# Modulation transfers on SyncE from the used weight tile, and one loop in the general path

## The chip, the cores and the metric

The kernel runs on one core of a Trainium2 chip. The metric is the device time of one execution in microseconds (us); the time shown is the median of three runs. All data are f32. Engines are named as in the profile: PE (TensorE), DVE (VectorE), ACT (ScalarE), POOL (GpSimd), SP (SyncE).

## What is computed

Two models in a row, on 256 tokens of width 1024. The first has two layers, each an attention mixer and a mixture of 16 experts (MoE). The second has one layer of another mixer and another MoE, and it is modulated by a vector c:

```python
mod = jax.nn.silu(c) @ w_ada[l] + b_ada[l]
sh1, sc1, g1, sh2, sc2, g2 = jnp.split(mod, 6, axis=-1)
h = _rms(x, norm1_g[l]) * (1.0 + sc1[:, None, :]) + sh1[:, None, :]
...
for e in range(N_EXPERTS):
    a = jax.nn.silu(h @ w_gate[e]) * (h @ w_up[e])
    y = y + dense_gates[:, e:e + 1] * (a @ w_down[e])
```

w_ada is 1024 x 6144. It needs c alone, so its product can be made at any time before the second model. Each expert has a gate and an up matrix of 1024 x 512 and a down matrix of 512 x 1024, 2 MB each, so a MoE loads 96 MB of weights. A token goes to two experts.

## The kernel before, in words

`run` (L1835) emits the program in this order: loads, then twice mixer (L572), router and `moe` (L955); then mixer2 (L1340), its router and `moe`. The order of the instructions on every engine is the order in which the Python code writes them.

**The weights.** Every weight load is a DMA issued by SP in `wload` (L109 to L115, the issue is L114). A `w` tile is 8 KB in each partition, 1 MB in all, and the pool has 13 of them; others come from pools r, b, 4 and 2. `moe_loads` cuts a MoE's weights into 96 jobs of 1 MB: by pairs of experts, gate, up and down, two halves of each expert. The function `load(upto)` issues the jobs that are not issued yet, up to a number. LATE (L35) is (3, 21): job 3, the second half of the gate of the first pair's second expert, is taken out of its place and becomes the 22nd; it comes as four pieces of 256 KB.

**Where the loads stand.** In a mixer, `filler` (L671) goes through the string FILL[l] (L30), one step at a time, between the units of attention:

```python
FILL = ("qkvcfgh5xaoAoAoAopppp", "qkvcfgh5xaoAoAoAoApppp")
MOE_FIRST = 22, 21
ADA_MX, ADA_TR = ((0, 1, 2, 3), (4, 6, 7, 8, 9), (11,)), (5, 10)
```

'5' is load(5), the first five expert jobs. 'x' loads the residual and the out projection's weights w_o, 'a' the further modulation weights `wa`, 'o' and 'p' are out projections (L541, into pout), and 'A' is one step of the modulation. In `moe`, load(MOE_FIRST[blk]) (L1014) issues the first 22 jobs (21 in the second model), as far as they are not issued; the general path (`overflow`) and load((0, 2)) follow. Then come eight pairs: expand (L1019, the products pz at L1026 with gate and up), shrink of the pair before (L1061, py at L1073 with down), gather and scatter, load((pr+1, 2)), and an ada step (L1119, L1120).

**The modulation.** `ada` (L1230 to L1263) makes w_ada's product in 12 blocks of 512 columns, each from two `wa` tiles. `rows(j)` (L1240) makes pada in PSUM; ACT copies pada to `part` (L1259, L1260), a tile of the m2 pool; `keep` (L1244) sends one row in 32 of part to a DRAM tile `ada`, by a DMA on the ACT queue (L1250). Once both halves of a segment are there, `column` (L1265) is put into a queue, and it reads the segment back as columns `adac` by another DMA on ACT's queue (L1268); `total` (L1271), on DVE, adds up and comes two ada steps after it. Blocks 0 to 3 belong to mixer 0: three by 'A', and the last in `run` by `next(fill, None)` (L1880), ahead of the call of `moe`. Block 5 comes after MoE 1, blocks 4, 6, 7, 8, 9 in mixer 1 (four by 'A' and the last at L1880), block 10 after MoE 2, block 11 in mixer2.

**The m2 pool.** It has five places of 2 KB in each partition (L81). `part` shares them with the softmax's E (written by ACT at L442), its transpose PT (L137), G (L975), sil, act, aT and the four pieces of job 3.

**The general path.** `overflow` (L1124) reads a flag that DVE made from the counts of tokens by expert. Only if an expert has more than 64 tokens does it go through all experts without the packing, in tiles lent by two of the loaded jobs, under the branch of L1128. In the profiled execution no instruction of that path ran, only the branch.

The functions that the change touches, and what calls them:

Of the kernel before, what the change touches and what calls it, by code (L numbers as in the profile page):

```python
# [10 lines left out]
F32 = mybir.dt.float32  # L11
# [4 lines left out]
AF = mybir.ActivationFunctionType  # L16
ALU = mybir.AluOpType
# [5 lines left out]
P = 128  # L23
# [24 lines left out]
class Net:  # L48
# [513 lines left out]
    def out_loads(self, src, pools, js):  # L562
# [7 lines left out]
        return t  # L570

    def mixer(self, l, hT, parts, W, ada, mid, tr, load):  # L572
        nc, c = self.nc, self.c

# [96 lines left out]
        def filler():  # L671
# [5 lines left out]
            for step in FILL[l]:  # L677
                if step in steps:
                    yield from steps[step]()
                    if step == "k" and l == 0:  # L680
                        self.tables2()
                    elif step == "f" and l == 0:
                        self.spread1()
                    elif step == "h" and l == 0:
                        self.spread2()
                elif step == "c":
                    fox_cum()
                    yield
                elif step == "a":
                    W["ada"] += self.ada_loads(ADA_MX[l][ADA_1[l]:])  # L690
                elif step in "123456789":
                    load(int(step))
                elif step == "x":
                    xt.append(self.unspill(xd, "xres"))
                    W["wo"] += self.out_loads(self.A["p_w_out"][l], OUT[0][0], OUT[0][2])
                elif step == "A":
                    next(ada, None)
                    yield
                else:
                    i = "op".index(step)  # L700
                    if not acc[i]:
                        acc[i] = [self.ps("pout", t) for t in ("aa", PT1)[i]]
                    for n in range(2):
                        self.out_mm(acc[i][n], oT, W["wo"], i, n, cc[i], cc[i] + 1)
                    cc[i] += 1
                    yield
# [417 lines left out]
    def overflow(self, parts, g, b, W, flag, gov, yacc, colscale, places, again):  # L1124

        nc, c = self.nc, self.c
        v = nc.values_load(flag[0:1, 0:1], min_val=0, max_val=1)
        with self.tc.If(v > 0):  # L1128
            govd = self.dp.tile([P, 32], F32, name="govd")
            nc.gpsimd.dma_start(govd, gov.rearrange("p i e -> p (i e)"))  # L1130
            for i in range(2):
                hT = [x.rearrange("p (k t) -> p k t", k=4) for x in places[:2]]
                for k in range(8):
                    pt = self.ps("opt", "t")
                    for n, part in enumerate(parts):
                        nc.tensor.matmul(pt[:, :P], part[:, i, k, :].bitcast(F32), c["ident"],
                                         start=(n == 0), stop=(n == 1))
                    self.evac(hT[k // 4][:, k % 4, :], pt[:, :P], g[:, k:k + 1], b[:, k:k + 1])
                with self.tc.For_i(0, 16) as e:
                    w3 = W(bass.ds(e, 1))  # L1140
                    gc = places[7][:, 0:1]
                    nc.gpsimd.dma_start(gc, govd[:, bass.ds(e + 16 * i, 1)])
                    pz = []
                    for n in range(2):
                        z = self.ps("oz", "a")
                        src = w3[n].rearrange("o (p k) f -> p (o k) f", k=8)
                        for k in range(8):
                            w = places[2 + k % 2]
                            nc.gpsimd.dma_start(w, src[:, k, :])
                            nc.tensor.matmul(z, hT[k // 4][:, k % 4, :], w, start=(k == 0), stop=(k == 7))  # L1150
                        pz.append(z)
                    a = places[4]
                    nc.scalar.activation(a, pz[0], AF.Silu)
                    nc.vector.tensor_mul(a, a, pz[1])
                    pa = self.ps("opa", "t")
                    for f in range(4):
                        nc.tensor.transpose(pa[:, f * P:(f + 1) * P], a[:, f * P:(f + 1) * P], c["ident"])
                    aT = places[5].rearrange("p (f t) -> p f t", f=4)
                    nc.scalar.activation(aT.rearrange("p f t -> p (f t)"), pa, AF.Copy)
                    src = w3[2].rearrange("o (c p) f -> p (o c) f", p=P)  # L1160
                    for n in range(2):
                        py = self.ps("opy", "o")
                        s = slice(n * 512, (n + 1) * 512)
                        for f in range(4):
                            w = places[2 + f % 2]
                            nc.gpsimd.dma_start(w, src[:, f, s])
                            nc.tensor.matmul(py, aT[:, f, :], w, start=(f == 0), stop=(f == 3))
                        if colscale is None:
                            nc.vector.scalar_tensor_tensor(yacc[:, i, s], py, gc, yacc[:, i, s], op0=ALU.mult,
                                                           op1=ALU.add)  # L1170
                        else:
                            t = places[6]
                            nc.vector.scalar_tensor_tensor(t, py, gc, colscale[:, s], op0=ALU.mult, op1=ALU.mult)
                            nc.vector.tensor_add(yacc[:, i, s], yacc[:, i, s], t)
            for t, src in again:
                nc.gpsimd.dma_start(t, src)
# [53 lines left out]
    def ada(self, blocks, W, tag="t", late=False):  # L1230


        nc, c = self.nc, self.c

        def rows(j):
            pa = self.ps("pada", tag)
            for k4 in range(2):
                w = W[2 * j + k4]
                for k in range(4):
                    nc.tensor.matmul(pa[32 * k:32 * k + 32, :], c["cz"][:, 4 * k4 + k:4 * k4 + k + 1].to_broadcast([P, 32]), w[:, k, :],  # L1240
                                     start=(k4 == 0), stop=(k4 == 1), tile_position=(0, 32 * k), skip_group_check=True)
            return pa

        def keep(b, part):  # L1244

            seg, n = divmod(b, 2)
            whole = seg in self.adad
            if not whole:
                self.adad[seg] = self.dp.tile([4, D], F32, name=f"ada{seg}")
            nc.scalar.dma_start(self.adad[seg][:, n * 512:(n + 1) * 512], part[::32, :])  # L1250
            if whole:
                self.adaq += [lambda: None, lambda: self.column(seg)]

        for j, b in enumerate(blocks):
            self.ada_step()
            pa = rows(j)
            if late:
                yield
            part = self.m2([P, 512], "part")  # L1259
            nc.scalar.activation(part, pa, AF.Copy)  # L1260
            keep(b, part)
            yield
        yield  # L1263

    def column(self, seg):  # L1265
        nc, c = self.nc, self.c
        r = self.adac[seg] = self.m1([P, 4, 8], "adac")
        nc.scalar.dma_start(r, self.adad[seg].rearrange("r (q k) -> q r k", k=8))  # L1268
        self.adaq += [lambda: None, lambda: self.total(seg)]

    def total(self, seg):  # L1271
# [808 lines left out]
```

## Time and profile before

| what | value |
|---|---|
| median of three runs | 1252.47 us (1248.62 to 1252.79) |
| profiled execution | 1256.93 us |
| its span | 1255.3 us |
| PE busy | 1168.0 us, 93% of the span |
| DVE, ACT, POOL busy | 515.8, 381.8, 223.6 us |
| mean granted clock of PE | 0.974 |
| moved by DMA | 395.51 MB, mean 315 GB/s |
| last scatter product of MoE 1 ends on PE | 406.85 us |
| branch L1128 on PE (three times) | 2.685, 6.027, 6.050 us |

The span is the profiled stretch of the execution; its own time is 1.6 us more. Times inside the execution count from the start of the span. "Granted clock" is the TensorE clock that the throttle granted, as a share of full speed. An "issue" is the instruction with which an engine hands a DMA to a queue; its landing comes later. In a row of a timeline, "x4" is the number of instructions of one kind that are put together, and the bracket tells how long the engine was idle ahead of the first and which event ended that.

### The profile page before, as it was taken

How to read it: one execution, taken by the hardware profiler on the slowest of the kernel's cores; microseconds unless marked ns; L12 is line 12 of the kernel's file. 1: busy time of each engine (PE TensorE's matmuls, PEld its weight loads, DVE VectorE, ACT ScalarE, POOL GpSimd, SP SyncE). 2: the span in 40 equal slices, each digit the busy share in tenths (PEclk: the TensorE clock that was granted, in tenths of full speed). 3: DMA queues.
4: the chain of work that ended last, by engine and by line, in shares of the span. 5: the costliest groups of instructions: out<-in, count | busy, mean ns of one | idle time of the engine just before them, and what ended most of it. 6: DMA issues, size and time to landing. Idle time of an engine off the chain costs nothing. (4 is left out here: it accounts for less than half of the span.)

```text
span 1255.3 us, 16639 instructions
## 1 busy us (share of the span) xinstructions
PE 1168.0 (93%) x6360; PEld 675.0 (54%) x6366; DVE 515.8 (41%) x1135; ACT 381.8 (30%) x799; POOL 223.6 (18%) x320
## 2 busy tenths in 40 slices
PE   5999798999999899987999999789899998999997
PEld 4877353434443788535344343388898553434432
DVE  6665342212222656425023221465886351223323
ACT  5544332111111655415011011356455431101100
POOL 4653200000000356200000000022564200000000
PEclk9999899999999999988999999989899998999999
DMA  9815939999999963757899999984344358999995
GB/s 384 353 40 210 384 116 368 415 411 404 415 417 413 390 245 135 306 198 277 344 373 417 414 414 416 417 337 166 108 169 155 147 226 314 415 415 415 415 417 231
DMA packets 80895, 395.51 MB, mean 315 GB/s; under 512 B 10760, under 2 KB 12528, under 8 KB 52384
## 3 DMA queue, kind: packets, MB, share of 16 engines
q1 hardware_dynamic: 73488, 384.66, 77.1%
q10 hardware_dynamic: 7312, 9.62, 2.2%
q8 instruction: 55, 0.90, 0.3%
q14 instruction: 40, 0.33, 0.1%
HBM read 389.41 MB, written 6.51 MB: 315 GB/s over the span
## 5 line engine op out<-in xcount | busy, mean ns | idle before, releaser
L1026 PE MATMUL pz<-we,xT 128*64 128x512 f32 x1536 | 342.3, 603 | 14.4 <-PEq L1128 13.2
L1026 PEld LDWEIGHTS pz<-we,xT 128*64 128x64 f32 x1536 | 111.0, 139 | 232.4 <-issue 223.8
L1073 PE MATMUL py<-wd,aT 128*64 128x512 f32 x768 | 173.3, 593 | 3.0 <-DMA wd<-in_exp_w_down 2.1
L1035 DVE TENSOR_TENSOR act<-sil,pz 128x512 f32<-128x512 f32 x24 | 16.5, 688 | 320.5 <-PE pz L1026 295.5
L1073 PEld LDWEIGHTS py<-wd,aT 128*64 128x64 f32 x768 | 55.5, 137 | 115.7 <-issue 106.5
L1050 POOL TENSOR_SCALAR m_ge<-m_s 64x1 f32<-64x1 f32 x48 | 11.9, 249 | 587.6 <-DVE m_s L1045 334.3
L1079 ACT ACTIVATE yh<-py,m_ge 128x512 fp32r<-128x512 f32 x32 | 22.0, 687 | 191.9 <-PE py L1073 191.9
L1030 ACT ACTIVATE sil<-pz 128x512 f32<-128x512 f32 x24 | 14.3, 597 | 210.9 <-PE pz L1026 202.1
L1080 DVE SCALAR_TENSOR_TENSOR yl<-py,m_ge,yh 128x512 fp32r<-128x512 f32 x32 | 24.0, 751 | 101.0 <-ACT yh L1079 101.0
L541 PE MATMUL pout<-w_o,oT 128*128 128x512 f32 x128 | 61.1, 627 | 4.7 <-ACT part L1260 4.7
L986 PE MATMUL pg<-G,xhi 128*128 128x256 f32 x192 | 47.8, 290 | 2.0 <-DVE G L975 2.0
L448 POOL TENSOR_SCALAR E<-E,r 128x128 f32<-128x128 f32 x40 | 30.7, 767 | 105.4 <-DVE r L444 101.6
L986 PE MATMUL pg<-G,xlo 128*128 128x256 f32 x192 | 46.7, 283 | 0.0
L541 PEld LDWEIGHTS pout<-w_o,oT 128*128 128x128 f32 x128 | 24.9, 203 | 32.7 <-issue 27.2
L1085 ACT ACTIVATE yh<-yf 128x512 fp32r<-128x512 f32 x16 | 10.1, 630 | 104.0 <-DVE yf L1084 104.0
L1099 PE MATMUL psc<-yh,GT 128*128 128x512 f32 x96 | 39.3, 410 | 1.1 <-ACT yh L1085 0.8
L1101 DVE TENSOR_TENSOR yacc<-yacc,psc 128x512 f32<-128x512 f32 x64 | 40.1, 680 | 0.0
L1099 PE MATMUL psc<-yl,GT 128*128 128x512 f32 x96 | 38.5, 401 | 1.3 <-DVE yl L1080 0.6
L986 PEld LDWEIGHTS pg<-G,xhi 128*128 128x128 f32 x192 | 36.7, 191 | 2.4 <-issue 1.6
L442 ACT ACTIVATE E<-s,nm 128x128 f32<-128x128 f32 (+1 forms) x48 | 20.2, 421 | 56.1 <-DVE nm L441 42.3
L986 PEld LDWEIGHTS pg<-G,xlo 128*128 128x128 f32 x192 | 36.8, 191 | 0.0
L291 PE MATMUL pt<-pk,xn 128*128 128x128 f32 x96 | 17.1, 337 | 12.3 <-ACT xn L132 12.2
(498 smaller groups left out, 2107.9 us busy)
## 6 DMA issues: line engine op xcount, KB each, us to landing
wd<-in_exp_w_down SPq DMA_DIRECT2D x58, 1024.0 KB, 12.7
we<-in_exp_w_up SPq DMA_DIRECT2D x54, 1024.0 KB, 11.9
we<-in_w SPq DMA_DIRECT2D x52, 1024.0 KB, 14.7
we<-in_exp_w_gate SPq DMA_DIRECT2D x48, 1024.0 KB, 13.9
wd<-in_w SPq DMA_DIRECT2D x29, 1024.0 KB, 17.3
wa<-in_p_ada SPq DMA_DIRECT2D x24, 1024.0 KB, 12.4
we<-in_exp_w_gate SPq DMA_DIRECT2D x28, 512.0 KB, 13.0
we<-in_w SPq DMA_DIRECT2D x22, 512.0 KB, 13.7
```

Of the source, the lines that this page charges most:

```text
L291: nc.tensor.transpose(pt[:, k * P:(k + 1) * P], xn[:, 4 * k4 + k, :], self.c["ident"])
L442: nc.scalar.activation(E[:, s], sc[:, s], AF.Exp, bias=nm[:, i:i + 1], accum_out=sm[:, i:i + 1])
L448: self.nc.gpsimd.tensor_scalar(E[:, 0:P], E[:, 0:P], r[:, 0:1], None, op0=ALU.mult)
L541: self.nc.tensor.matmul(acc, oT[:, cc, i * P:(i + 1) * P], w[cc][:, n * 512:(n + 1) * 512], start=(cc == 0), stop=(cc == 7), skip_group_ch ...
L986: nc.tensor.matmul(pg[:, :256], part[:, i, k, :], Gq[q][:, i].rearrange("p e s -> p (e s)"), start=(n == 0), stop=(n == 3))
L1026: nc.tensor.matmul(pz[64 * e:64 * e + 64, :], x[:, k, o + 64 * e:o + 64 * e + 64], w[e][k], start=(k == 0), stop=(k == 7), skip_group_chec ...
L1035: nc.vector.tensor_mul(a, st[pr].pop("sil"), pz)
L1073: nc.tensor.matmul(py[n][64 * e:64 * e + 64, :], aT[:, f, 64 * e:64 * e + 64], w[e][f][:, n * 512:(n + 1) * 512], start=(f == 0), stop=(f ...
L1079: nc.scalar.activation(yh[:, s], py[n], AF.Copy, scale=ge)
L1080: nc.vector.scalar_tensor_tensor(yl[:, s], py[n], ge, yh[:, s].bitcast(F32), op0=ALU.mult, op1=ALU.subtract)
L1099: nc.tensor.matmul(pt, GT[:, i * P:(i + 1) * P], y[:, s], start=(j == 0), stop=(j == 1), skip_group_check=True)
L1101: nc.vector.tensor_tensor(yacc[:, i, s], yacc[:, i, s], pt, op=ALU.add)
```

## The change

Three edits. In the general path the loop over the experts takes both tiles of tokens in its body, where before it was written out once for each; the tokens' parts are added by DVE first and then transposed. In `ada` the copied product goes into the first of the four 512-wide rows of the second `wa` tile that `rows` has just used, where before it had an m2 tile of its own. And keep's and column's DMAs are issued by SP, where before ACT issued them.

```diff
@@ overflow @@
+            for i in range(2):
+                for j in range(2):
+                    k = slice(4 * j, 4 * j + 4)
+                    nc.vector.tensor_tensor(x[2 * i + j], parts[0][:, i, k].bitcast(F32), parts[1][:, i, k].bitcast(F32),
+                                            op=ALU.add)
             for i in range(2):
-                hT = [x.rearrange("p (k t) -> p k t", k=4) for x in places[:2]]
                 for k in range(8):
                     pt = self.ps("opt", "t")
-                    for n, part in enumerate(parts):
-                        nc.tensor.matmul(pt[:, :P], part[:, i, k, :].bitcast(F32), c["ident"],
-                                         start=(n == 0), stop=(n == 1))
...
-                with self.tc.For_i(0, 16) as e:
-                    w3 = W(bass.ds(e, 1))
-                    gc = places[7][:, 0:1]
-                    nc.gpsimd.dma_start(gc, govd[:, bass.ds(e + 16 * i, 1)])
+                    nc.tensor.transpose(pt[:, :P], x[2 * i + k // 4][:, k % 4, :], c["ident"])
...
+            gc = self.sp.tile([P, 2, 1], F32, name="m_gc", bufs=1)
+            with self.tc.For_i(0, 16) as e:
+                w3 = W(bass.ds(e, 1))
+                nc.gpsimd.dma_start(gc, govd.rearrange("p (i e) -> p i e", i=2)[:, :, bass.ds(e, 1)])
+                for i in range(2):
...
@@ keep @@
-            nc.scalar.dma_start(self.adad[seg][:, n * 512:(n + 1) * 512], part[::32, :])
+            nc.sync.dma_start(self.adad[seg][:, n * 512:(n + 1) * 512], part[::32, :])
@@ ada @@
-            part = self.m2([P, 512], "part")
+            part = W[2 * j + 1][:, 0, :]
             nc.scalar.activation(part, pa, AF.Copy)
@@ column @@
-        nc.scalar.dma_start(r, self.adad[seg].rearrange("r (q k) -> q r k", k=8))
+        nc.sync.dma_start(r, self.adad[seg].rearrange("r (q k) -> q r k", k=8))
```

## Rows read from the trace of the kernel before

**Rows 1.** Windows: busy us of PE, PEld, DVE, ACT, POOL; clock, DMA share, GB/s

```profile
118.00:153.00 35.00, 26.11 (x132) 12.56 (x131) 10.47 (x32) 10.48 (x35) 7.53 (x11) 0.89 0.98 393
...
300.00:400.00 100.00, 100.00 (x486) 40.56 (x484) 23.38 (x45) 13.71 (x21) 1.91 (x8) 1.00 1.02 412
700.00:804.00 104.00, 101.46 (x482) 40.91 (x478) 26.50 (x52) 14.48 (x22) 1.91 (x8) 1.00 1.02 415
```

**Rows 2.** Waits: engine, line, releaser, total us, times, longest

```profile
ACT E L442 <- DMA ada<-part: 21.0, 5, 8.2
...
PE pz L1026 <- PEq L1128: 13.2, 3, 5.6
```

**Rows 3.** Timeline of ACT: start, us, work, [idle before, releaser]

```profile
134.78 0.37 ACT L442 ACTIVATE E<-sd,nm 128x128 f32<-128x128 f32 x1 [8.24 <-DMA ada<-part]
...
191.94 0.51 ACTq L1250 DMA_DIRECT2D ada<-part  x1
...
584.43 0.49 ACTq L1250 DMA_DIRECT2D ada<-part  x1
```

**Rows 4.** Timeline of PE, five windows, same columns

```profile
137.82 1.22 PE L525 MATMUL hss<-hsq,bones 128*128 128x256 f32 x2 [6.06 <-ACT hsq L516]
...
141.11 2.22 PE L1240 MATMUL pada<-wa,cz 128*32 128x512 f32 x16
...
150.68 0.52 PE L455 MATMUL ptp<-pk,E 128*128 128x128 f32 x3 [1.85 <-DVE PT L137]
...
199.88 6.12 PE L1026 MATMUL pz<-we,xT 128*64 128x512 f32 x18 [2.17 <-PEq L1128]
206.95 5.37 PE L1026 MATMUL pz<-we,xT 128*64 128x512 f32 x24 [0.94 <-DMA we<-in_exp_w_gate]
...
542.22 6.53 PE L541 MATMUL pout<-w_o,oT 128*128 128x512 f32 x8 [4.71 <-ACT part L1260]
...
595.63 15.68 PE L1026 MATMUL pz<-we,xT 128*64 128x512 f32 x64 [5.43 <-PEq L1128]
```

**Rows 5.** Windows after two stops of PE

```profile
149.00:156.00 7.00, 5.32 (x20) 3.19 (x21) 3.23 (x10) 2.80 (x11) 1.51 (x2) 0.76 0.97 350
542.20:549.00 6.80, 6.78 (x10) 3.04 (x11) 1.69 (x6) 1.79 (x6) 1.30 (x2) 0.58 0.97 351
```

**Rows 6.** Timeline of SP (DMA issues) in mixer 0

```profile
115.60 3.09 SPq L114 DMA_DIRECT2D wa<-in_p_ada  x4
120.93 13.46 SPq L114 DMA_DIRECT2D we<-in_exp_w_up  x2
```

**Rows 7.** Tile views, landing: we (43 to 60), wa (114 to 196)

```profile
DMA to landing us min/median/max: 5.0/5.1/5.1
...
DMA to landing us min/median/max: 23.3/23.3/23.3
```

**Rows 8.** DMA from 120.5 to 191.8: GB/s in slices, issues

```profile
GB/s 439 414 439 421 409 425 418 421 267 313 386 432 418 411 404 363 359 301 395 345 379 216 101 7 9 0 0 0 0 0 0 0 64 322 202 106 381 414 421 412
...
wd<-in_exp_w_down SPq DMA_DIRECT2D x4, 1024.0 KB, 9.6
we<-in_exp_w_up SPq DMA_DIRECT2D x3, 1024.0 KB, 14.4
we<-in_exp_w_gate SPq DMA_DIRECT2D x3, 1024.0 KB, 13.4
we<-in_exp_w_up SPq DMA_DIRECT2D x6, 512.0 KB, 4.6
we<-in_exp_w_gate SPq DMA_DIRECT2D x4, 512.0 KB, 12.2
```

**Rows 9.** Lines of PE: busy us, mean ns, idle before, releasers

```profile
L1073 PE MATMUL py<-wd,aT 128*64 128x512 f32 x768 | 173.3, 593 | 3.0 <-DMA wd<-in_exp_w_down 2.1 <-DMA wd<-in_w 0.9
```

**Rows 10.** Timeline of SP in mixer2

```profile
911.78 29.50 SPq L114 DMA_DIRECT2D we<-in_w  x6
960.94 0.81 SPq L404 DMA_DIRECT2D xtok<-xd  x2
```

More of the change, by code (lines that the diff above doesn't have):

```diff
@@ L1130, in overflow @@
             nc.gpsimd.dma_start(govd, gov.rearrange("p i e -> p (i e)"))
+            hT = [x.rearrange("p (k t) -> p k t", k=4) for x in places[:4]]
+            x = [y.rearrange("p (k t) -> p k t", k=4) for y in places[4:]]
             for i in range(2):
-                hT = [x.rearrange("p (k t) -> p k t", k=4) for x in places[:2]]
+                for j in range(2):
[3 more added lines that the diff above has]
+            for i in range(2):
                 for k in range(8):
                     pt = self.ps("opt", "t")
-                    for n, part in enumerate(parts):
-                        nc.tensor.matmul(pt[:, :P], part[:, i, k, :].bitcast(F32), c["ident"],
-                                         start=(n == 0), stop=(n == 1))
-                    self.evac(hT[k // 4][:, k % 4, :], pt[:, :P], g[:, k:k + 1], b[:, k:k + 1])
-                with self.tc.For_i(0, 16) as e:
-                    w3 = W(bass.ds(e, 1))
-                    gc = places[7][:, 0:1]
-                    nc.gpsimd.dma_start(gc, govd[:, bass.ds(e + 16 * i, 1)])
+                    nc.tensor.transpose(pt[:, :P], x[2 * i + k // 4][:, k % 4, :], c["ident"])
+                    self.evac(hT[2 * i + k // 4][:, k % 4, :], pt[:, :P], g[:, k:k + 1], b[:, k:k + 1])
+            gc = self.sp.tile([P, 2, 1], F32, name="m_gc", bufs=1)
[3 more added lines that the diff above has]
+                for i in range(2):
                     pz = []
@@ L1147, in overflow @@
                         for k in range(8):
-                            w = places[2 + k % 2]
+                            w = places[4 + k % 2]
                             nc.gpsimd.dma_start(w, src[:, k, :])
-                            nc.tensor.matmul(z, hT[k // 4][:, k % 4, :], w, start=(k == 0), stop=(k == 7))
+                            nc.tensor.matmul(z, hT[2 * i + k // 4][:, k % 4, :], w, start=(k == 0), stop=(k == 7))
                         pz.append(z)
-                    a = places[4]
+                    a = places[6]
                     nc.scalar.activation(a, pz[0], AF.Silu)
@@ L1157, in overflow @@
                         nc.tensor.transpose(pa[:, f * P:(f + 1) * P], a[:, f * P:(f + 1) * P], c["ident"])
-                    aT = places[5].rearrange("p (f t) -> p f t", f=4)
-                    nc.scalar.activation(aT.rearrange("p f t -> p (f t)"), pa, AF.Copy)
+                    nc.scalar.activation(a, pa, AF.Copy)
                     src = w3[2].rearrange("o (c p) f -> p (o c) f", p=P)
@@ L1164, in overflow @@
                         for f in range(4):
-                            w = places[2 + f % 2]
+                            w = places[4 + f % 2]
                             nc.gpsimd.dma_start(w, src[:, f, s])
-                            nc.tensor.matmul(py, aT[:, f, :], w, start=(f == 0), stop=(f == 3))
+                            nc.tensor.matmul(py, a[:, f * P:(f + 1) * P], w, start=(f == 0), stop=(f == 3))
                         if colscale is None:
-                            nc.vector.scalar_tensor_tensor(yacc[:, i, s], py, gc, yacc[:, i, s], op0=ALU.mult,
+                            nc.vector.scalar_tensor_tensor(yacc[:, i, s], py, gc[:, i], yacc[:, i, s], op0=ALU.mult,
                                                            op1=ALU.add)
                         else:
-                            t = places[6]
-                            nc.vector.scalar_tensor_tensor(t, py, gc, colscale[:, s], op0=ALU.mult, op1=ALU.mult)
+                            t = places[7]
+                            nc.vector.scalar_tensor_tensor(t, py, gc[:, i], colscale[:, s], op0=ALU.mult, op1=ALU.mult)
                             nc.vector.tensor_add(yacc[:, i, s], yacc[:, i, s], t)
```

## The prediction, on record before the result

> **What bounds the kernel now.** I read the stretches of the span first. In both MoE stages PE is busy all the time and the DMA engines are too: 100.00 us of 100 with 412 GB/s from 300 to 400, 101.46 of 104 with 415 GB/s from 700 to 804 [rows 1]. So a MoE stage has no slack to catch up in: what delays its start is paid in full at its end. The attention of mixer 0 is another case: from 118 to 153 PE was busy 26.11 of 35 us [rows 1].
>
> Second, the waits. ACT's softmax write of E waited five times, 21.0 us in all, 8.2 at the longest, for the landing of ada<-part [rows 2]: E and `part` share the m2 pool, so E gets its place only when keep's transfer out of an old `part` has landed.
>
> Third, PE's timeline. It stood 6.06 us until hss (released by ACT's hsq, which ran behind the 8.24 us wait of E), then 1.85 us, and in mixer 1 4.71 us ahead of pout [rows 3, 4]. After the stops the clock was low: 0.76 of full from 149 to 156 and 0.58 from 542.2 to 549 [rows 5].
>
> Last, SP's timeline. SP takes its instructions in the order in which the program writes them, and is far ahead of the others: the next MoE weight load goes out at 120.93, right behind the four loads of modulation weights, 71 us ahead of the last block's keep on ACT (191.94) [rows 3, 6].
>
> **The change: the part in the weight tile.** The copy into the used tile waits for PE's last read of it, as it waited for pada before: 0. `part` no longer takes an m2 place, so ACT's wait of E goes, and with it the ACT queue's hold at keep. In mixer 0 the gain is not the whole 6.06: the third block's pada, at 141.11, needs its wa tiles [rows 4]. The four wa loads were issued from 115.60, and one is seen to land 23.3 us after its issue [rows 6, 7]; the last issue of that group begins at 118.4, so the fourth lands at about 141.7, and at 2.545 us a load (1.0486 MB at 412 GB/s) the second, which the third block wants, at about 136.6. That part gains 141.11 - 136.6 = 4.5; the 1.85 goes; and the clock's share is 5.32 us of PE work x (1 - 0.76) = 1.3 [rows 4, 5]. Together 7.7. In mixer 1: 4.71, and 6.78 x (1 - 0.58) = 2.8 of low clock [rows 4, 5], together 7.5. Bounds for each: 0, if the stop only moves, and 10, if the second-order gaps go too.
>
> **The change: keep and column on SP.** 18 issues of about 0.5 us each [rows 3] leave ACT and come to SP; neither engine is the bound, so the issues themselves count 0 (at most 9 us of ACT's time, which lies beside PE's work). The price is the order. In mixer 0 the filler string emits load(5), then x, a, and the steps A; the fourth block comes at L1880, and load(MOE_FIRST), which brings the first 22 jobs, stands only behind it in `moe` (L1014). So of the 22 jobs five are ahead of the keeps on SP, and 17 behind all four. A keep waits on SP until ACT has written that block's part, and whatever is behind it on SP waits too. The fourth part is ready when its keep was issued before, at 191.94 [rows 3]. The work that was issued meanwhile, from 120.5 to 191.8, is 4 + 3 + 3 loads of 1 MB and 6 + 4 of half a MB, 15 MB [rows 8]; all this, and the two jobs after it, now starts behind the fourth keep.
>
> Who waits for it: job 3, the last quarter of the first pair's gate weights, is by LATE the 22nd loaded. Expand(0,0) did 18 matmuls from 199.88, and went on at 206.95 when job 3's first piece came [rows 4]. After: keep 4 at 191.94 - 7.7 = 184.2. The first load behind it lands after 5.0 us (an undisturbed load [rows 7]), each further MB after 2.545, so the first quarter of the 17th, 15.25 MB further, after 5.0 + 38.8 = 43.8: at 228.0. Against 206.95 that is +21.1. PE has then stood for some 30 us; the low clock after it costs what the 18 matmuls at 199.88 paid: 6.12 us, against 18 x 5.37/24 = 4.0 at full clock [rows 4], so +2.1. Together **+23.2**, and nothing of it is won back, since from there on PE has the same work with the same 22 jobs landed; the remaining 74 loads need 188 us, less than PE's 200 from 206.95 to the end of the stage's products (406.85, the table).
>
> MoE 2 likewise: keep 584.43 - 7.5 = 576.9, job 3's first piece at 620.7. Before, PE ran 64 matmuls from 595.63 in 15.68 us without a stop; its last 46 at 5.37/24 take 10.3, so the 18th ended at 601.0 [rows 4]. That is +19.7, and +2.1 for the clock. As all 22 jobs are then in place, the 2.1 us for which py waited for its down weights [rows 9] may go: **+19.7** in all.
>
> Bounds of the hold: the 17 loads can't come at more than the best slice's 439 GB/s [rows 8] (2.39 us a load, 2.4 us less per stage), nor at less than about the 393 GB/s of the first mixer stretch [rows 1] (2 us more). Clock: 0 to 4 us per stage.
>
> **Small parts.** In mixer2 the last block's keep and column come to stand ahead of six expert loads on SP. Those went out from 911.78 to 941.3, and SP's next issue was at 960.94 [rows 10]: some 20 us of slack cover a start that is 10 us later. I take 0, and 5.0, one landing [rows 7], if that cover is gone. The weight slot that is held until keep has landed is wanted by loads far ahead of their use, which lie under the same slack: 0, or one landing of 5.0 if one is late. DVE's total finds the column landed before, as it comes two ada steps later: 0. The general path isn't taken; only its branch shows, 13.2 us in three waits, 5.6 the longest [rows 2]. In MoE 1 and 2 it now lies under the wait for job 3; in MoE 3 a shorter body may save something between 0 and 3, a longer one for some engine may cost as much; I take 0.
>
> **The sum.** 1256.93 + 23.2 + 19.7 = 1299.8 for the profiled execution. That one stands 4.46 above the median of the runs, so **1295.3**.
>
> One rule of the Trainium skill speaks against this. By the page "Trainium Kernel Development and Optimization", section Key Constraints, transfers issued from the SP, ACT and POOL queues run on the same 16 DMA engines and interleave, and issuing from several engines only saves issue time. By it alone the move is nearly free, and the sum would be the gains only, which is the first rival; the rows on SP's order [rows 6] say what the rule leaves out, that an issue waits behind its queue's earlier waits.
>
> **The rivals.**
> *Faster:* SP is not held by the fourth keep, as its place on SP falls behind load(MOE_FIRST). The third block's keep would then release SP about when its pada ends, some 143, and 17 MB from there need 43.8 us, up to 187, ahead of expand(0,0). Then the gains stand alone: 7.7 + 7.5 + 0.9 that PE waited for job 3 [rows 4] = 16, so 1236. It decides if the keep of the fourth block is issued after the first loads behind it. Against it: L1880 comes ahead of L1014 in the text, and SP's loads ran in the order of the text throughout [rows 6]. 0.06.
> *No change:* the same, but E's wait in ACT is taken over by another holder of the m2 places (G, PT, act), so that nothing is gained: about 1250. For it speaks that five m2 places serve many tiles; against it that the wait names the landing of ada<-part each time [rows 2]. 0.05.
> *Held and no gain:* SP held as forecast, but the stops in the mixers only move, as PE then waits for wa or w_o, which is near in mixer 0. Then 15.2 comes on top: 1310.5. 0.08.
> *Clock in the MoE stages:* after the late start loads land just ahead of their use, and PE stops at some pairs; each stop that lowers the clock costs 2.1 [rows 4] plus itself. With one such in every second pair of two stages, 8 x 2.1 = 17, so 1312 and up. Against it: the 22 jobs landed at the restart are the same lead as before, and there was one stop of 2.1 us in both stages [rows 9]. 0.06. The page "TensorE: Matmul & The Clock Gate", section "HAM oscillation — how this bites in real kernels", tells of a kernel that fell back to the low clock at each wait for DMA; the trace shows low clock after long stops only in part [rows 5].
>
> **How the numbers follow.** The forecast has 0.75, with 1295.3. Its own bounds: faster stream 4.8, larger gains 4.8 and no cost of the clock 4.2 take it down to about 1281; slower stream 4, gains halved 7.6 and 2 more of clock per stage up to 1310. With the rival "held and no gain" taken in, and something for a hold shorter than I think, the range is 1277 to 1311. A measurement of this kernel can tell about 0.5% (6.3 us) from no change. Faster 0.06; same 0.05; slower 0.75 + 0.08 + 0.06 = 0.89.
>
> **What would show it.** Right: SP's timeline has no load from about 119 (520 in mixer 1) to 184 (577); the DMA share there falls to near 0 and is then 1.0 for 44 us; PE waits at pz for in_exp_w_gate some 30 us near 200 and some 25 us near 595; ACT's waits of E for ada<-part are gone, and the stops before hss and pout are shorter. Wrong: loads of expert weights on SP between 125 and 180; pz without a long wait; PE's end of MoE 1 before 415. If E's waits are there under another name, the gain is at fault; if the waits at pz are much shorter than 20 us, the hold is.

## The result, and the profile after

The changed kernel took 1298.34 us (median of five runs) against 1252.47 before: a ratio of 1.036 with a 95% interval of 1.0334 to 1.0385, slower by about 46 us. The forecast was 1295.3. One of the five runs was disturbed from end to end (2394 us), and it was the one with the profile, so the profile below is from a second run of the same kernel (1297.22 us, ratio 1.0363, interval 1.0329 to 1.0397; its profiled execution 1296.82, span 1295.2 against 1255.3).

The windows of the changed kernel, with one that reaches from the last keep of mixer 0 to PE's restart:

```profile
118.00:153.00 35.00, 31.07 (x150) 14.90 (x149) 13.94 (x42) 13.89 (x46) 9.18 (x14) 0.90 0.56 228
153.00:192.00 39.00, 37.00 (x186) 23.09 (x186) 20.21 (x55) 16.38 (x25) 3.33 (x9) 0.96 0.13 48
185.00:231.00 46.00, 10.94 (x58) 6.19 (x56) 4.93 (x20) 3.82 (x6) 0.79 (x2) 0.67 0.98 386
300.00:400.00 100.00, 100.00 (x504) 43.22 (x502) 25.56 (x49) 14.58 (x24) 1.90 (x8) 1.00 1.02 415
```

Against [rows 1], PE is busier in the attention (31.07 of 35 us where it was 26.11): the gain forecast for the tile. But the DMA engines moved 228 GB/s there, and 48 from 153 to 192. From 185 to 231 they are full and PE has 10.94 us of work in 46. From 300 to 400 all is as it was.

SP's timeline, mixer 0 and then mixer 1, and what its keeps waited for show why; they answer to [rows 6]:

```profile
116.17 3.06 SPq L114 DMA_DIRECT2D wa<-in_p_ada  x4
121.82 17.80 SPq L1254 DMA_DIRECT2D ada<-wa  x3
141.78 0.39 SPq L1272 DMA_DIRECT2D adac<-ada  x1
185.30 0.50 SPq L1254 DMA_DIRECT2D ada<-wa  x1
185.85 0.91 SPq L114 DMA_DIRECT2D we<-in_exp_w_up  x2
186.81 3.48 SPq L114 DMA_DIRECT2D we<-in_exp_w_gate  x6
...
538.38 10.57 SPq L114 DMA_DIRECT2D wa<-in_p_ada  x4
...
557.22 44.98 SPq L1254 DMA_DIRECT2D ada<-wa  x3
602.29 0.87 SPq L114 DMA_DIRECT2D we<-in_exp_w_up  x2
...
SPq L1254 <- ACT wa L1264: 84.8, 5, 43.0
```

Between 142.2 and 185.3 SP issues nothing: it stands for 43.0 us at the fourth keep, for which ACT has no data yet. The first expert load goes out at 185.85, where it went out at 120.93. In mixer 1 the same: the last of the three keeps that begin at 557.22 is issued at 601.7, and the load behind it at 602.29.

PE's timeline at the first pz of MoE 1 and MoE 2, and at the end of both stages; it answers to [rows 4]:

```profile
194.11 5.89 PE L1026 MATMUL pz<-we,xT 128*64 128x512 f32 x18 [3.03 <-PEq L1128]
231.14 5.31 PE L1026 MATMUL pz<-we,xT 128*64 128x512 f32 x16 [31.14 <-DMA we<-in_exp_w_gate]
...
434.38 1.92 PE L1244 MATMUL pada<-wa,cz 128*32 128x512 f32 x16 [2.23 <-DVE yacc L1101]
...
611.12 7.29 PE L1026 MATMUL pz<-we,xT 128*64 128x512 f32 x18 [3.62 <-PEq L1128]
647.88 4.29 PE L1026 MATMUL pz<-we,xT 128*64 128x512 f32 x12 [29.46 <-DMA we<-in_exp_w_gate]
...
851.24 2.64 PE L1244 MATMUL pada<-wa,cz 128*32 128x512 f32 x16 [2.23 <-DVE yacc L1101]
```

PE comes to MoE 1 earlier than before (194.11 against 199.88), does the same 18 matmuls, and then stands 31.14 us for job 3, where it stood 0.94. A stage's products end at the pada row less its idle time: 432.15 and 849.01, where it was 406.85 (409.08 less 2.23) and 804.13. So MoE 1 ends 25.3 us late and MoE 2 44.9 us late; the end of the span is 39.9 us late.

### The profile page after: what moved, and what is told of

Same layout as the page of the kernel before. It is cut to its first block, busy times and chain, and to the rows that moved or that the text cites. A ratio compares the mean times of both kernels' runs of the same rounds, so it can differ in the third digit from the quotient of the medians.

```text
span 2392.3 us, 16638 instructions
## 1 busy us (share of the span) xinstructions
PE 2309.1 (97%) x6360; PEld 1097.2 (46%) x6366; DVE 514.9 (22%) x1135; ACT 390.8 (16%) x799; POOL 216.8 (9%) x320
## 5 line engine op out<-in xcount | busy, mean ns | idle before, releaser
L1026 PE MATMUL pz<-we,xT 128*64 128x512 f32 x1536 | 725.0, 1147 | 56.0 <-DMA we<-in_exp_w_gate 53.0
L1026 PEld LDWEIGHTS pz<-we,xT 128*64 128x64 f32 x1536 | 150.0, 187 | 601.7 <-issue 531.8
L1073 PE MATMUL py<-wd,aT 128*64 128x512 f32 x768 | 363.7, 1148 | 0.0
L541 PE MATMUL pout<-w_o,oT 128*128 128x512 f32 x128 | 122.3, 1151 | 0.0
L986 PE MATMUL pg<-G,xhi 128*128 128x256 f32 x192 | 84.1, 451 | 2.0 <-DVE G L975 2.0
L986 PE MATMUL pg<-G,xlo 128*128 128x256 f32 x192 | 82.2, 441 | 0.0
L1099 PE MATMUL psc<-yh,GT 128*128 128x512 f32 x96 | 68.4, 712 | 0.4 <-ACT yh L1085 0.4
L986 PEld LDWEIGHTS pg<-G,xlo 128*128 128x128 f32 x192 | 65.6, 342 | 0.0
L986 PEld LDWEIGHTS pg<-G,xhi 128*128 128x128 f32 x192 | 63.9, 333 | 3.0 <-issue 1.6
L1244 PE MATMUL pada<-wa,cz 128*32 128x512 f32 x192 | 46.4, 1132 | 2.1 <-DVE yacc L1101 2.1
```

The costliest lines, as they stand in the source:

```text
L541: self.nc.tensor.matmul(acc, oT[:, cc, i * P:(i + 1) * P], w[cc][:, n * 512:(n + 1) * 512], start=(cc == 0), stop=(cc == 7), skip_group_ch ...
L986: nc.tensor.matmul(pg[:, :256], part[:, i, k, :], Gq[q][:, i].rearrange("p e s -> p (e s)"), start=(n == 0), stop=(n == 3))
L1026: nc.tensor.matmul(pz[64 * e:64 * e + 64, :], x[:, k, o + 64 * e:o + 64 * e + 64], w[e][k], start=(k == 0), stop=(k == 7), skip_group_chec ...
L1073: nc.tensor.matmul(py[n][64 * e:64 * e + 64, :], aT[:, f, 64 * e:64 * e + 64], w[e][f][:, n * 512:(n + 1) * 512], start=(f == 0), stop=(f ...
L1099: nc.tensor.matmul(pt, GT[:, i * P:(i + 1) * P], y[:, s], start=(j == 0), stop=(j == 1), skip_group_check=True)
```

## The experiments

All ratios are against the kernel before, run on the same chip; intervals are 95%. The first run is the changed kernel once more, whose profile is above.

> The changed kernel once more, for an undisturbed profile: about 1298 us. If SP's order is the price: no expert load on SP from about 119 to 184 and from 520 to 577, PE waits at pz for in_exp_w_gate until about 228 and about 644 (the latter with MoE 1's delay of 23 added), MoE 1's products end near 430. Rival, the MoE stages are slowed inside (clock or single DMA waits): pz waits under 10 us each, and the two stages from the first pz on take over 8 us longer than before.

It came as the first theory says, with restarts 3 to 4 us later than expected: 1297.22 us, restarts at 231.1 and 647.9, and no stop at pz inside the stages.

### The tile without the queue, the queue without the tile

The first keeps the transfers on ACT's queue, the second keeps the m2 tile. Both have the general path of before.

```diff
-            part = self.m2([P, 512], "part")
+            part = W[2 * j + 1][:, 0, :]
```

> Part in the weight tile, transfers still issued by ACT, general path as before. If the order on SP is the whole price and the tile's gain is real: loads at their old times, E's waits for ada<-part gone, 1236 us (7.7 + 7.5 + 0.9 less than 1252.5); 1240 if the ACT queue is still held at keep by DMA waits. Rival, the stops only move: 1250 to 1254. Rival, the held weight tile delays the loads: above 1255.

```diff
-            nc.scalar.dma_start(self.adad[seg][:, n * 512:(n + 1) * 512], part[::32, :])
+            nc.sync.dma_start(self.adad[seg][:, n * 512:(n + 1) * 512], part[::32, :])
...
-        nc.scalar.dma_start(r, self.adad[seg].rearrange("r (q k) -> q r k", k=8))
+        nc.sync.dma_start(r, self.adad[seg].rearrange("r (q k) -> q r k", k=8))
```

> Keeps and columns on SP, part in its own m2 tile, general path as before. By the sum the hold alone, with the attention's stops left as they were: 1252.5 + 42.9 + 15.2 = 1310 us. If E's waits were due to ACT's own queue rather than to the m2 place, they go here too: 1295. If the hold isn't the price: under 1275.

The tile alone: 1250.36 us, ratio 0.9984 (0.9967 to 1.0002). It gained 2 us, not clear of zero, and not 16, so here the rival was right: the stop only moved. The queue alone: 1310.61, ratio 1.0459 (1.0427 to 1.049), 58 us of price where 1310 was expected. That it fits to the microsecond is in part luck: the sum has 30.9 us for MoE 1 (23.2 + 7.7) and 27.2 for MoE 2 (19.7 + 7.5), and the stages ended 35.7 us late and another 22.3. Waits and PE's stop of the tile-only kernel, then the waits of ACT and of SP's keep in the queue-only kernel:

```profile
ACT E L442 <- DMA t5d<-t5s: 13.0, 1, 13.0
...
137.88 1.54 PE L466 MATMUL pod<-PT,dall 128*64 128x256 f32 x6 [10.13 <-DVE PT L137]
```

```profile
ACT E L442 <- DMA ada<-part: 17.5, 1, 17.5
...
SPq L1250 <- ACT part L1260: 85.6, 5, 41.5
```

In the tile-only kernel the m2 wait is gone, but E now stands 13.0 us behind a keep on ACT's own queue, and that keep waits until t5d, a transfer that ACT issued earlier, has landed. PE's stop in mixer 0 is 10.13 us, longer than the 6.06 of [rows 4]. At the first pz PE then stood 5.81 us for job 3, where it stood 0.94, and MoE 1 ended 5.8 us later than before; why these loads came later was not tried by itself. Mixer 1 has no such transfer, and there the gain came with keep still on ACT's queue: from the end of MoE 1 (412.60) to that of MoE 2 (800.35) are 387.8 us, against 397.3 before. So in mixer 0 the tile does not pay while all keeps stay on ACT's queue (a run below moves one of them), and the two edits are not a plain sum: on top of the queue edit the tile, with the general path's edit beside it, is worth 13.4 us (1310.6 to 1297.2), by itself 2. In the queue-only kernel E still waits for a keep, 17.5 us at once, as the m2 place is shared; and SP stands at keeps for 85.6 us in all, 41.5 at the longest: that is the hold.

### Which keep holds the loads

With the tile and the general path of before, first only the last keep ahead of each MoE on ACT and all else on SP, then the reverse.

```diff
+            eng = nc.scalar if b in (3, 9) else nc.sync
+            eng.dma_start(self.adad[seg][:, n * 512:(n + 1) * 512], part[::32, :])
```

> Part in the weight tile, all keeps and columns on SP except the keeps of block 3 and block 9, the last ahead of each MoE, which ACT issues; general path as before. If it is the last keep alone that holds the 17 loads back: SP is free at about 143 and 535, job 3 lands before PE wants it, 1236 to 1240 us. Rival, each keep or column on SP costs its part: between 1260 and 1290.

```diff
+            eng = nc.sync if b in (3, 9) else nc.scalar
+            eng.dma_start(self.adad[seg][:, n * 512:(n + 1) * 512], part[::32, :])
```

> Part in the weight tile, only the keeps of blocks 3 and 9 on SP, all others and the columns on ACT, general path as before. If the last keep alone holds the loads: two stops at pz of 25 to 31 us, and as ACT's queue is held in mixer 0 as in the tile-only kernel, 1297 + about 6 = 1303 us. Rival, the hold is the sum of several keeps: 1260 to 1285.

The reverse gave 1302.45 (1.0354 to 1.0423), where 1303 was expected: the two last keeps alone bring the whole delay, with stops at pz of 33.7 and 28.5 us. The first gave 1255.39 (0.9996 to 1.0041), not the 1236 to 1240 expected and outside of the rival's range too: MoE 1 ended 13.3 us later than the kernel before, and the stretch from there to the end of MoE 2 was 10.6 us shorter. Its SP timeline in mixer 0, SP's wait, and PE's stop:

```profile
143.04 0.93 SPq L114 DMA_DIRECT2D we<-in_exp_w_up  x2
144.07 4.63 SPq L114 DMA_DIRECT2D we<-in_exp_w_gate  x6
188.50 4.25 SPq L114 DMA_DIRECT2D we<-in_exp_w_up  x7
...
SPq L114 <- DMA ada<-wa: 45.5, 2, 39.8
...
219.38 3.42 PE L1026 MATMUL pz<-we,xT 128*64 128x512 f32 x8 [20.94 <-DMA we<-in_exp_w_gate]
```

SP is free at 143 as expected, issues eight loads, and then waits 39.8 us for the landing of ada<-wa, although that keep was now issued by ACT (at 186.75). In the built program the transfers of SP and ACT take turns on eight completion semaphores, which tell that a transfer has landed, and the ninth load waits for one thing only: the semaphore that the keep raises. So a transfer can hold another queue's transfer without standing in it. In mixer 1 there is no such long wait, and PE has no stop for job 3.

Another link could be the place of the used weight tile, which is not free until keep has read it. The kernel with all keeps on POOL, further below, speaks against that. It has the part in the same tile and the loads in the same order, and there SP issues the loads behind the eighth from 145.00 on, while that keep goes out at 185.77 (SP, then POOL):

```profile
145.00 31.38 SPq L114 DMA_DIRECT2D we<-in_exp_w_up  x7
...
185.77 0.63 POOL L1250 DMA_DIRECT2D ada<-wa  x1
```

That the semaphore is the cause was read from the wait, the program and this comparison; no run changed the turn by itself.

### Bytes or job 3

The changed kernel with job 3 as the sixth load of the first two MoE stages:

```diff
-LATE = (3, 21), (3, 20)
+LATE = (3, 5), (3, 20)
```

> The changed kernel with job 3 as the sixth load of MoE 1 and MoE 2 instead of the 22nd. If the missing bytes are the price, PE starts some 30 us earlier, then stops again and again for loads, and the stage ends when the stream does: 185.3 + 5.0 + 90 loads x 2.545 + a tail of 8.2 = 427.5 for MoE 1 against 432.2, so about 1288 us in all. Rival, it is job 3's late place that costs, not the bytes: PE goes on from 200 without the 31 us stop, and 1250 to 1260 us.

It gave 1292.93 (1.0285 to 1.0349), 5 us over the 1288 expected: 4 us better than the changed kernel, with intervals that overlap. PE's first pz is not followed by a long stop, and instead PE waits 34 times for down weights in the two stages (waits, and PE's timeline at the start and end of MoE 1):

```profile
PE py L1073 <- DMA wd<-in_exp_w_down: 34.0, 34, 1.7
...
191.61 8.80 PE L1026 MATMUL pz<-we,xT 128*64 128x512 f32 x40 [1.25 <-PEq L1128]
...
431.43 1.92 PE L1244 MATMUL pada<-wa,cz 128*32 128x512 f32 x16 [2.23 <-DVE yacc L1101]
```

MoE 1 ends at 429.2 where the stream of loads gave 427.5. It is the missing 17 MB that cost, and in the changed kernel job 3 only decides whether they are paid for in one stop or in many.

### The general path alone

The edit of `overflow` as in the change, with the modulation as before.

> The general path as one loop, the modulation as before. If it costs nothing: 1252 us, within 3; the three waits behind the branch (2.2, 5.4, 5.6 us) somewhat shorter as PE's body is shorter, the last by up to 2. Rival, the other body costs at the branch: 1256 or more.

1250.91 us, ratio 0.9975 (0.9956 to 0.9993): a gain of 2 us. Its branch stops (waits of PE):

```profile
PE pz L1026 <- PEq L1128: 4.7, 2, 2.4
...
PE pz L1026 <- DMA we<-in_w: 5.3, 1, 5.3
```

In [rows 2] the branch cost 13.2 us in three stops. Now it is 4.7 in two; MoE 2's fell from 5.43 to 2.33. The third stop, in MoE 3, stays at 5.3, only under the name of a load: the weights were not there sooner.

### The order put right

The changed kernel with the loads up to the 18th emitted ahead of the last block, so that SP has 13 of them in front of the keep that waits longest:

```diff
             self.to_tok(h1T, yacc[:, 1, :], 1, ALPHA, "a", "s")
+            loads[0](18)
             next(fill, None)
```

> The changed kernel with load(18) emitted ahead of the last modulation block in each of the first two layers, so that 13 loads stand on SP ahead of the keep that waits longest. If SP's order is the whole price and the tile's gain is real: no long stop at pz, 1235 to 1243 us, faster than both kernels. Rival, the attention's gain is lost again in the MoE stage as the loads can't come sooner: 1248 to 1253. Rival, the order isn't the price: 1290 or more.

1240.54 us, ratio 0.9894 (0.9862 to 0.9926); in the repeat

> The kernel with load(18) ahead of the last block once more, beside the next three on one chip: 1238 to 1243 us.

1238.61, ratio 0.9873 (0.9843 to 0.9903). One line takes away 57 us, and the kernel is faster than both. SP's timeline and PE's restart of the first of the two runs:

```profile
121.21 18.58 SPq L1254 DMA_DIRECT2D ada<-wa  x3
139.88 1.58 SPq L114 DMA_DIRECT2D we<-in_exp_w_up  x2
141.52 3.31 SPq L114 DMA_DIRECT2D we<-in_exp_w_gate  x6
145.16 27.70 SPq L114 DMA_DIRECT2D we<-in_exp_w_up  x7
173.29 11.06 SPq L114 DMA_DIRECT2D wd<-in_exp_w_down  x3
...
185.47 0.51 SPq L1254 DMA_DIRECT2D ada<-wa  x1
...
202.10 3.68 PE L1026 MATMUL pz<-we,xT 128*64 128x512 f32 x8 [5.66 <-DMA we<-in_exp_w_gate]
```

The loads begin at 139.88, 19 us later than in [rows 6], behind the third keep; that costs nothing to be seen, since SP waited for free places in between anyway: in the kernel with the keeps on POOL they begin at 121.42, and job 3's first piece comes no sooner, at 203.14 against 202.10. The fourth keep comes at 185.47, with the loads ahead of it. PE still stands 5.66 us for job 3, so that MoE 1 ends at 404.09, only 2.8 us sooner than in the kernel before; the greater part of the gain, 11.3 us, comes between there and the end of MoE 2.

Two other ways around the hold, both with the tile and the general path of before: only block 1's keep on SP, or all keeps and columns on POOL.

```diff
+            eng = nc.sync if b == 1 else nc.scalar
...
-            nc.scalar.dma_start(self.adad[seg][:, n * 512:(n + 1) * 512], part[::32, :])
+            nc.gpsimd.dma_start(self.adad[seg][:, n * 512:(n + 1) * 512], part[::32, :])
```

> Part in the weight tile, only the keep of block 1 on SP (there SP waits for the landing of t5d in any case), all others and the columns on ACT, general path as before. If ACT's queue waiting for t5d is what ate the tile's gain in mixer 0: PE's 10 us stop near 128 goes, 1238 to 1245 us. Rival, ACT is held by the next keep instead: 1247 to 1252.

> Part in the weight tile, keeps and columns on POOL's queue, general path as before. If neither order on SP nor ACT's queue is in the way: 1238 to 1245 us. Rival, POOL's waits for ACT's part hold its share of the softmax: stops of PE in the attention come back, 1248 to 1256.

1241.97 (0.9883 to 0.9935) and 1243.58 (0.9901 to 0.9951). PE's first pz with block 1's keep on SP:

```profile
192.19 4.50 PE L1026 MATMUL pz<-we,xT 128*64 128x512 f32 x18 [0.69 <-ACTq L1128]
```

The tile-only kernel comes there at 200.37, and the end of MoE 1 is 404.36 against its 412.60. Block 1's keep is thus the one that kept the tile from paying in mixer 0. POOL waits 12.2 us in four waits for ACT's part, and an issue takes it 0.62 us, without a stop of PE for it in the attention. The intervals of the three ways overlap, and only the first of them has the general path's 2 us in it.

Last, the order put right and job 3 as the 18th load:

```diff
-LATE = (3, 21), (3, 20)
+LATE = (3, 17), (3, 20)
```

> The kernel with load(18) ahead, and job 3 as the 18th load in MoE 1 and MoE 2 (ahead of the last block's keep) instead of the 22nd. If each MoE ends when its stream does (PE's end 8.1 us behind the last down weight's landing): the 5.7 us stop at the first pz goes and comes back as waits for later loads, 1237 to 1242 us. Rival, job 3 is what ends last: 11 us less, 1229.

1231.22 us, ratio 0.9828 (0.9802 to 0.9855): the best kernel of the study, 1.7% below the kernel before. It is 7.4 us less than the repeat on the same chip, where the first theory had next to nothing and the rival 11: nearer to the rival. PE's waits and its timeline at the start and end of MoE 1:

```profile
PE py L1073 <- DMA wd<-in_exp_w_down: 2.2, 2, 1.2
...
192.76 12.67 PE L1026 MATMUL pz<-we,xT 128*64 128x512 f32 x58 [2.33 <-PEq L1128]
...
399.70 2.79 PE L1244 MATMUL pada<-wa,cz 128*32 128x512 f32 x12 [2.24 <-DVE yacc L1101]
```

The stop of 5.66 us went, and the down weights cost 2.2 us in two waits, 1.2 of them in MoE 1. My theory had taken the 8.1 us between the last down weight's landing and PE's end for a sign that the stream sets the end. But the loads wait for places that PE frees, so that the stream follows PE as long as its lead lasts: MoE 1 ends at 397.46 here, against 404.09 with job 3 late. The DMA engines moved 412 GB/s from 190 to 390, against 402 in the same window there.

## Why the prediction was right, step by step

**The hold** was right in place and size. Keep 4 was forecast at 184.2 and issued at 185.30. From there to job 3's first piece 43.8 us were forecast and 45.8 passed in MoE 1 (231.14), 46.2 in MoE 2 (647.88 less 601.72): half a us from the keep to the first load, and the rest because 16 loads came at some 2.64 us each rather than 2.545. That is about the 2 us that the bounds allow for a slower stream; the window from 185 to 231 has 386 GB/s, with 0.85 us in it ahead of the first load. The delay of the first restart is 24.2 us instead of 21.1. That the last keep alone does it, the reverse experiment shows. That the time is not won back within the stage is in the ends of the stages.

**The clock** after the stop cost less than its term of 2.1: from restart to the end of MoE 1 201.0 us passed, against 199.9 before, so 1.1. The windows show 0.67 of full clock over the stretch from 185 to 231, mostly while PE stood. For MoE 1 the two errors together give +25.3 instead of +23.2. MoE 2 added 19.6, and 19.7 were forecast, with the gain in mixer 1 nearly right (from MoE 1's end to the last keep 169.6 us against 177.6, so 8.0 for 7.5), a longer hold, and a branch stop of 3.6 for 5.4 under it.

**The tile's gain** in mixer 0 was 6.6 (191.94 less 185.30) for 7.7. The bound by wa held: PE waited for these weights, while the stop of 6.06 us ahead of hss in [rows 4] is gone (the last line has all that hss still waits):

```profile
134.15 1.06 PE L1244 MATMUL pada<-wa,cz 128*32 128x512 f32 x8 [1.89 <-DMA wa<-in_p_ada]
136.52 1.94 PE L1244 MATMUL pada<-wa,cz 128*32 128x512 f32 x8 [1.30 <-DMA wa<-in_p_ada]
...
PE hss L525 <- ACT hsq L516: 1.0, 2, 0.5
```

The second tile came at 136.5, estimated at 136.6. ACT's E waits for no transfer any more, and the stop of 4.71 us ahead of pout in mixer 1 is gone too. What the prediction did not see is that in mixer 0 this gain needs block 1's keep off ACT's queue: with all keeps on it the 13.0 us behind t5d take its place. Its rival "faster", with the tile's gains alone, named 1236, near the kernel with the order put right (1238.6 and 1240.5), while the tile without the queue stayed at 1250. The nearness is in part luck: of the 8.6 us that the rival has ahead of the end of MoE 1 (7.7 + 0.9) only 2.8 are there, and 11.3 where it has 7.5.

**The small parts.** At the end of the kernel the forecast took 0, and 5.0 us came back: mixer2, from the end of MoE 2 to where PE stops ahead of MoE 3's first pz, took 227.2 us against 230.6, and MoE 3 some 1.8 less. In mixer2 the windows show PE busy 209.71 us against 212.24 with the same work. The change need not be the cause. In the thirteen profiled executions of all these kernels that stretch took 227.2 to 230.6 us: the kernel before has the longest, the changed kernel the shortest, and the last experiment, which has the change in it too, 230.5. What sets it in one execution stays open. The general path was taken at 0 and is worth 2 us alone (expected from 0 to 3); in the changed kernel that is under the stops for job 3 in MoE 1 and 2.

**The sum** was 3 us under the median (1295.3 for 1298.34) and 3 us over the profiled execution (1299.8 for 1296.82). By stage it had 23.2 for 25.3, 19.7 for 19.6, and 0 for the 5.0 that came back behind MoE 2. The 4.46 that the prediction takes off belongs to the one execution of the kernel before that was profiled, so how close the two times came owes something to which executions these were; the two holds, within 2.1 us by stage, do not.

Of the rivals, "held and no gain" at 1310.5 has the time of the queue-only kernel at 1310.6. "Clock in the MoE stages" did not come: no stop at pz inside the stages of the changed kernel. By the page "Trainium Kernel Development and Optimization" of the Trainium skill, section Key Constraints, issuing from several engines at once saves only issue time; the queue-only kernel, 58 us slower with the same transfers, speaks against taking it for the whole story.

## What to carry to other kernels

Before a transfer is moved to the queue that loads weights, look at what stands behind it there, and for how long the engine that makes its data will be late: the price is the prefetch that this queue would have issued meanwhile, bytes over bandwidth, and it is paid in full where the next stage has no slack. Putting the loads ahead in the program is one line and turned 3.6% slower into 1.1% faster. Then ask what a freed resource allows: here the load that PE waited for, which has places in the m2 pool that `part` had left, could come earlier, for another 7 us. Whether it needs `part` out of that pool was not tried.

## What the runs showed that was not expected

A transfer waited, ahead of its issue, for the landing of another whose data it does not need: 39.8 us a load on SP for a keep that ACT had issued, and 13.0 us a keep on ACT for t5d, which ACT itself had issued. The order of the queues alone does not tell this. And a tight tie between the last load and the end of a stage, 8.1 to 8.2 us in MoE 1 of all but one of these kernels (7.8 with the tile alone), did not mean that the loads set the end.
